# Weight buffers of 4096 bytes in place of 4288, and one input block of the mixer in three pieces in place of two

## The chip, the cores and the metric

The kernel runs on one core of a Trainium2 chip, in one launch. The metric is the device time of one execution in microseconds (us). The kernel before has three timed runs, with a median of 2028.21 us (2024.9 to 2028.38).

## The reference

Two layers of a streaming encoder work on 512 tokens of 1024 features, all in float32. A layer has three sublayers: a SwiGLU feed-forward step (FFN), a mixer, and a second FFN. In front of each sublayer the input is shifted and scaled by vectors that come from a conditioning vector `c`; behind each comes a gated residual and a LayerNorm.

```python
for l in range(DEPTH):                                   # DEPTH = 2
    h = modulate(x, mod[:, 0, 0], mod[:, 0, 1])
    y = swiglu_ffn(h, ffn1_w_in[l], ffn1_w_out[l])       # 1024 -> 2 x 2816 -> 1024
    x = layer_norm(ALPHA * x + 0.5 * mod[:, 0, 2] * y, ln_g[l, 0], ln_b[l, 0])
    h = modulate(x, mod[:, 1, 0], mod[:, 1, 1])
    proj = h @ mix_w_in[l]                               # 1024 -> 3084 columns
    ...                                                  # scan | attention | short convolution
    y = jnp.concatenate([y_ssd, y_fox, y_sc], axis=-1) @ mix_w_out[l]
    x = layer_norm(ALPHA * x + mod[:, 1, 2] * y, ln_g[l, 1], ln_b[l, 1])
    h = modulate(x, mod[:, 2, 0], mod[:, 2, 1])
    y = swiglu_ffn(h, ffn2_w_in[l], ffn2_w_out[l])
    x = layer_norm(ALPHA * x + 0.5 * mod[:, 2, 2] * y, ln_g[l, 2], ln_b[l, 2])
```

## The kernel before

**Products in three parts.** Every large operand is held as two float32r parts, a high one and a low one (the rest). One block of a product is three matmuls, in the helper `mm3`: the low part of the stationary operand by the high part of the moving one, then high by low, then high by high. The names tell the parts: `hi` and `li` are the high and low part of an FFN input weight, `ho` and `lo` of an output weight, `hm...` and `lm...` of a mixer weight, `hh` and `hl` of the sublayer's transposed input, `ah` and `al` of the FFN's activations.

Two kinds of product make up most of the work. In the input products (`pf` in the FFN, `pj...` in the mixer) the stationary operand is a 128x128 block of weights, and the moving one is 512 columns of `hh` or `hl`. The three matmuls of a block are, in this order, `pf<-hh,li`, `pf<-hl,hi` and `pf<-hh,hi` (the name behind the arrow is the moving operand, the last one the stationary). Eight blocks, 24 matmuls, fill one accumulator of 512 columns; I call these 24 a run of products. In the output products (`po`) and the gate of the mixer (`pz`) it is the other way round: the stationary operand is a block of the activations (or of `hh`, `hl`), the moving one 512 columns of weights: `po<-ho,al`, `po<-lo,ah`, `po<-ho,ah`. In the first pair of a later FFN and in two of the mixer's projections (`b`, `c`) a matmul has only 256 columns.

**Weights.** `load` (line 395) brings 1 MB of raw weights into one of two buffers (`rawp`); `split` (line 407) makes the high part on ScalarE (ACT) and the low part on VectorE (DVE), for one half of the block at a time, into one of six buffers of the pool `whp` and one of six of `wlp`. The six are taken in turn, so a new half waits until the products that read the half six places earlier are through. `WSZ` (line 35) is the number of float32 words of such a buffer: 1072, or 4288 bytes per partition. A half of a usual block needs 1024 words. The 1072 words are needed in one place: at the head of the mixer the columns of v, forget gate and dt (268 in all) are loaded in two pieces of 4 x 268 words each (lines 790 to 806, products `pv`).

**Where the operands lie.** All buffers are laid one behind the other in SBUF in the order of the pools. In the built program of the kernel before, the places per partition, modulo 512 bytes, are:

| operand | place of its buffers modulo 512 |
|---|---|
| `whp`, buffers 0 to 5 (`hi`, `ho`, `hm`) | 448, 128, 320, 0, 192, 384 |
| `wlp`, buffers 0 to 5 (`li`, `lo`, `lm`) | 64, 256, 448, 128, 320, 0 |
| `hh`, `hl`; `ah`, `al`; the other long-lived tiles | 192 |

The blocks inside a buffer lie at multiples of 512 bytes from its start, so that a matmul's operand has the place of its buffer. A low part lies 128 bytes behind its high part, modulo 512, in every pair of buffers. In pair 4 the high part has the place of `hh`, `hl`, `ah` and `al`; in pair 0 it lies 256 bytes from it, and in pairs 5, 3, 2 and 1 at 192, 320, 128 and 448 bytes behind it.

**Order.** TensorE (PE) runs its instructions in the order of the program, mostly that of the code; adaLN work (`ra`, `acc`) is spread between the weight units by `tick`. SyncE (SP) issues all loads of weights in order.

Of the kernel before, what the change touches and what calls it, by code (L numbers as in the profile page):

```python
# [15 lines left out]
P = 128  # L16
# [17 lines left out]
CR = (2.7, 1.3)  # L34
WSZ = 1072

# [5 lines left out]
class InOrder:  # L42
    """An engine whose instructions are issued in program order while it is on."""

# [16 lines left out]
def issue_after(tc, ins, prev):  # L61
    """Issue order on one engine."""
    tc.add_manual_dep(ins.ins, prev.ins.name,
                      mybir.DependencyInfo(mybir.DependencyClass.NoSync, mybir.DependencyReason.DATA),
                      reason="issue order")
# [3 lines left out]
def trunk(ctx, tc, x, c, ln_in_g, ln_in_b, ada_w, ada_b, ffn1_w_in, ffn1_w_out,  # L69
# [6 lines left out]

    const = ctx.enter_context(tc.tile_pool(name="const", bufs=1))
    rawp = ctx.enter_context(tc.tile_pool(name="rawp", bufs=2))
    adap = ctx.enter_context(tc.tile_pool(name="adap", bufs=2))
# [31 lines left out]

# [1 line left out]
    ident = const.tile([P, P], F32, name="ident")  # L113
# [4 lines left out]
    pool.memset(mhalf, -0.5)  # L118
# [1 line left out]
    cT = const.tile([P, KD], F32, name="cT")  # L120
# [32 lines left out]
    def columns(dst, rows):  # L153
        """[n, 128] to [128, n]."""
        n = rows.shape[0]
        ps = pb([P, n], f"pv_{dst.tensor.name}")
        pe.transpose(ps, rows, ident[0:n, 0:n])
        dve.tensor_copy(dst, ps)

# [1 line left out]
    identb = const.tile([P, P], BF16, name="identb")  # L161
# [51 lines left out]

# [1 line left out]
    gates = {}  # L215
# [6 lines left out]
    def ada_acc(l, col):  # L222
        """acc[p, f] = sum_k silu(c)[8p + k] * ada_w[l, 8p + k, col + f], row by row."""
        w = ada_w[l].rearrange("(p k) f -> p k f", k=KD)
# [15 lines left out]
    def acc_split(acc):  # L240
        """The high and low part of each half."""
        parts = []
        los = adap.tile([P, 2, 512], F32R, tag="ra", name="gl")
        for h in range(2):
            hi, lo = tmp([P, 512], "gh", F32R), los[:, h]
            act.activation(hi, acc[h], AF.Copy)
            dve.tensor_tensor(lo, acc[h], hi.bitcast(F32), ALU.subtract)
            parts.append((hi, lo))
        return parts

    def acc_sum(ps, hi, lo):
        """The sum over the partitions, on every partition."""
        pe.matmul(ps, onesr, hi, start=True, stop=False)
        pe.matmul(ps, onesr, lo, start=False, stop=True)
# [5 lines left out]
    def mod_finish(s, a, b, psc, pss):  # L260
        """Features a*128 to b*128: scale and shift folded with the LayerNorm in front."""
        l, j = divmod(s, 3)
# [38 lines left out]
    def ada_first(part, which):  # L301
        """The row blocks of the first sublayer's scale (1) or shift (0) for one range of features."""
        w = ada_w[0].rearrange("(p k) f -> p k f", k=KD)
# [13 lines left out]
    def sum_first(part, raws):  # L317
        """The sums over the row blocks, one vector instruction at a time."""
        n = FIRST[part][1] * P
# [50 lines left out]
    def begin(*gens):  # L370
        """Queue background work, to be spread over the 33 weight units of a half-step FFN."""
        pending.extend(gens)
        credit[0] = 0.0
        credit[1] = len(pending) and CR[0] if len(gens) > 2 else CR[1]
# [17 lines left out]

# [1 line left out]
    def load(w, c0, r0, k, n, name):  # L394
        """Rows r0 to r0 + 128 k, columns c0 to c0 + n, as [128, k, n]."""
        raw = rawp.tile([P, 2048], F32, tag="raw", name="r" + name)
# [6 lines left out]
    def split(v, name, prev=None):  # L403
        """One half unit, any view [128, a, b] of raw weights, as high and low parts."""
        a, b = v.shape[1], v.shape[2]
# [6 lines left out]
    def cols_unit(w, c0, name, prev=None):  # L412
        """256 columns of a [1024, .] matrix, two halves [128, 8, 128]."""
        v = load(w, c0, 0, KD, 256, name)
        return [split(v[:, :, j * P:(j + 1) * P], f"{name}_{j}", prev) for j in range(2)]

    def rows_unit(w, r0, c0, nk, name, prev=None):
        """128 nk rows by 512 columns, halves [128, 2, 512]."""
        v = load(w, c0, r0, nk, 512, name)
# [7 lines left out]

# [1 line left out]
    def ln_stat(t, h, st, piece=None):  # L429
        """Statistics of 512 columns, or of one half of them."""  # L430
        n = 2 * 512 // st.shape[1]
# [16 lines left out]
    def finish(t, st):  # L448
        """The last LayerNorm, stored."""
        mu, rs = ln_mr(st)  # L450
# [8 lines left out]
    def ln_norm(t, st):  # L459
        """xt[t] <- (xt[t] - mean) * rstd."""  # L460
        mu, rs = ln_mr(st)
# [4 lines left out]
    def modulate(s, t, qq=(0, 1), prev=None):  # L466
        """hT[:, :, t] = the transposed modulation of xt[t] for sublayer s."""
        ts = slice(t * P, (t + 1) * P)
# [22 lines left out]
    def modulate_first(kk, ps):  # L491
        """hT[:, kk, :] for the first sublayer; yields before the vector part."""
        hf = tmp([P, T], f"hf0_{kk}")
# [9 lines left out]
    def ln_in(t):  # L503
        """The first LayerNorm of one token tile; yields between its vector parts."""
        ln_stat(t, 0, st0[t])
# [9 lines left out]
    def start():  # L515
        """Up to the first pair of the first sublayer, by ranges of features."""
        for e in (pe, dve, act):
# [108 lines left out]
    def x_affine(s, eng):  # L626
        """xt = normalized * g + b of the LayerNorm in front of sublayer s."""
        ln_vectors(s)
# [6 lines left out]
    def fold(s, ps, t, h, first, half, a=0, b=512):  # L635
        """xt[t][:, h] <- (alpha *) xt + gate * (1/2) * ps, columns a to b."""
        hs = slice(h * 512 + a, h * 512 + b)
# [11 lines left out]

# [1 line left out]
    def by_token(ah, al):  # L651
# [52 lines left out]
    def out_proj(s, w_out, r0, acts, half, first, last):  # L704
        """x <- (alpha *) x + gate * (acts^T w_out); with last, on to the next sublayer's input."""
        n = len(acts)
# [43 lines left out]

# [1 line left out]
    def mixer(s, l):  # L752
        w_in, w_out = mix_w_in[l], mix_w_out[l]

        def feat(c0, name, epi, halves=False, between=None):
            """256 projected features, feature-major; epi(chunk, psum)."""
            us = cols_unit(w_in, c0, name)
# [31 lines left out]

        # v, forget-gate and dt columns together, token-major  # L790
        us = []
        for u in range(2):
            raw = rawp.tile([P, 2048], F32, tag="raw", name=f"rm{s}v{u}")
            v = raw[:, 0:4 * 268].rearrange("p (k f) -> p k f", f=268)
            rs = slice(u * 512, (u + 1) * 512)
            sp.dma_start(v[:, :, 0:260], w_in[rs, C_V:C_V + 260].rearrange("(k p) f -> p k f", p=P))
# [3 lines left out]
        for t in range(NT):  # L800
            ts = slice(t * P, (t + 1) * P)
            ps = pa([P, 268], f"pv{s}_{t}")
            for k in range(KD):
                wh, wl = us[k // 4]
                mm3(ps, hT[0][:, k, ts], hT[1][:, k, ts], wh[:, k % 4, :], wl[:, k % 4, :],
                    k == 0, k == KD - 1)
# [32 lines left out]

        # sums within a 128-token chunk: up to the token, of the whole chunk, after the token  # L840
        def decays(prev):
# [8 lines left out]

            # forget gate: minus its running sum, one row per head
            psf = pb([P, NT, 4], f"pcf{s}")
# [21 lines left out]

        # B token-major
        btok = []
# [9 lines left out]

        # token-major x * dt and x * d
        xdt, xd = [], []
# [13 lines left out]

        # gate z, token-major
        zs = []
# [22 lines left out]
        def ssd_decay(i):  # L927
            """M[s, e, l] = (C_l . B_s) exp(sum of a over s < . <= l) for l >= s, per group."""
            ts = slice(i * P, (i + 1) * P)
# [21 lines left out]
        def ssd_state(i):  # L951
            """The state after chunk i: [n, h, d]."""
            xw = tmp([P, 8, 64], f"xw{s}_{i}")
# [54 lines left out]

        # forgetting attention
        qT = [slot([P, 2, 256], F32, f"q{s}_{u}") for u in range(2)]  # L1010
# [6 lines left out]
        def k_epi(j, ps):  # L1017
            """Per head: the high part twice, and the low part over minus the sums of the forget gate."""
            for p in range(2):
# [11 lines left out]
        def attn(i):  # L1031
            """One block of 128 queries, two stages for each head."""
            n = (i + 1) * P
# [47 lines left out]

        # gated short convolution
        cS, uS, gT = [], [], []
# [56 lines left out]

# [1 line left out]

# [42 lines left out]
```

## Time and profile before

| | |
|---|---|
| median of three runs | 2028.21 us (2024.9 to 2028.38) |
| span of the profiled execution, first to last instruction | 2026.3 us |
| PE busy | 1980.4 us (98%) in 9462 matmuls |
| DVE, ACT, POOL busy | 1190.0 us, 688.5 us, 218.2 us |
| share of PE in the chain that ended last | 85% |
| granted TensorE clock, mean | 0.998 |

The page gives no time of the profiled execution beside its span. The span lies 1.9 us under the median of the timed runs and within their range. Matmuls are pipelined: the duration of one in the profile (some 390 ns) is longer than the distance from its start to the next one's (some 230 ns), so the pace is read from stretches with a known number of matmuls. The names in the profile leave out buffer numbers; which buffer a stretch uses follows from counting the halves through the six buffers in the order of the program.

### The profile page before, as it was taken

How to read it: one execution, taken by the hardware profiler on the slowest of the kernel's cores; microseconds unless marked ns; L12 is line 12 of the kernel's file. 1: busy time of each engine (PE TensorE's matmuls, PEld its weight loads, DVE VectorE, ACT ScalarE, POOL GpSimd, SP SyncE). 2: the span in 40 equal slices, each digit the busy share in tenths (PEclk: the TensorE clock that was granted, in tenths of full speed). 3: DMA queues.
4: the chain of work that ended last, by engine and by line, in shares of the span. 5: the costliest groups of instructions: out<-in, count | busy, mean ns of one | idle time of the engine just before them, and what ended most of it. 6: DMA issues, size and time to landing. Idle time of an engine off the chain costs nothing.

```text
span 2026.3 us, 23498 instructions
## 1 busy us (share of the span) xinstructions
PE 1980.4 (98%) x9462; PEld 1624.8 (80%) x9462; DVE 1190.0 (59%) x1728; ACT 688.5 (34%) x1092; POOL 218.2 (11%) x182
## 2 busy tenths in 40 slices
PE   5999999999999999999999999999999999999998
PEld 4777878898877888888898788888977798888887
DVE  8896663467666655543477757436666575433336
ACT  3332132164454422122152322323544453222220
POOL 0230000007000040000004000000350004000000
PEclk9999999999999999999999999999999999999999
DMA  9765552333211544432345746322322144223331
GB/s 322 232 208 208 177 166 73 95 92 117 83 63 53 182 155 158 149 106 92 104 162 173 240 157 235 104 84 81 122 80 73 53 137 136 102 84 103 104 104 42
DMA packets 178540, 263.98 MB, mean 130 GB/s; under 512 B 9612, under 2 KB 124672, under 8 KB 178432
## 3 DMA queue, kind: packets, MB, share of 16 engines
q1 hardware_dynamic: 173936, 254.97, 37.7%
q10 hardware_dynamic: 4496, 7.52, 1.2%
q8 instruction: 74, 1.21, 0.2%
q14 instruction: 34, 0.28, 0.0%
HBM read 260.37 MB, written 2.10 MB: 130 GB/s over the span
## 4 chain that ended last, share of the span: by engine, by line
PE 85%; DVE 7%; DMA 4%; ACT 2%; issue 1%; POOL 0%; POOLq 0%; SPq 0%; DVEq 0%; ACTq 0%
PE pf L52 42%; PE po L52 26%; DMA ra<-in_ada_w_dram 4%; DVE acc L52 2%; PE pz L52 2%; PE pv L52 1%; PE pfo L52 1%; PE ptr L52 1%; DVE li L52 1%; PE pjm1x L52 1%; PE pS L52 1%; DVE af L52 1%; PE py L52 1%; PE pjm1sx L52 1%; PE pjm4sx L52 1%
## 5 line engine op out<-in xcount | busy, mean ns | idle before, releaser
L52 PE MATMUL pf<-hh,li 128*128 128x512 f32 (+1 forms) x1504 | 574.5, 382 | 1.3 <-DVE li L52 1.0
L52 PE MATMUL pf<-hl,hi 128*128 128x512 f32 (+1 forms) x1504 | 571.2, 380 | 0.2 <-DVE hl L52 0.2
L52 PE MATMUL pf<-hh,hi 128*128 128x512 f32 (+1 forms) x1504 | 570.7, 379 | 0.0
L52 DVE TENSOR_TENSOR li<-ri,hi 128x1024 fp32r<-128x1024 f32 x176 | 224.0, 1278 | 187.4 <-ACT hi L52 187.2
L52 PEld LDWEIGHTS pf<-hh,li 128*128 128x128 f32 x1504 | 283.3, 188 | 58.5 <-DVE li L52 1.7
L52 PEld LDWEIGHTS pf<-hl,hi 128*128 128x128 f32 x1504 | 284.8, 189 | 56.1 <-DVE hl L52 0.8
L52 PEld LDWEIGHTS pf<-hh,hi 128*128 128x128 f32 x1504 | 283.5, 188 | 57.7
L52 ACT ACTIVATE hi<-ri 128x1024 fp32r<-128x1024 f32 x176 | 185.4, 1059 | 317.4 <-PE pf L52 203.7
L52 PE MATMUL po<-ho,al 128*128 128x512 f32 (+1 forms) x704 | 276.6, 393 | 0.0
L52 PE MATMUL po<-ho,ah 128*128 128x512 f32 (+1 forms) x704 | 275.3, 391 | 0.0
L52 PE MATMUL po<-lo,ah 128*128 128x512 f32 (+1 forms) x704 | 274.7, 390 | 0.0
L52 DVE TENSOR_TENSOR lo<-ro,ho 128x1024 fp32r<-128x1024 f32 x104 | 127.2, 1223 | 215.3 <-ACT ho L52 215.2
L52 ACT ACTIVATE ho<-ro 128x1024 fp32r<-128x1024 f32 x104 | 110.1, 1058 | 293.1 <-PE po L52 166.6
L52 DVE SCALAR_TENSOR_TENSOR acc<-ra,cT,acc 128x512 f32<-128x512 f32 x224 | 171.6, 810 | 62.2 <-DMA ra<-in_ada_w_dram 61.9
L445 POOL TENSOR_TENSOR rs<-ve,mhalf 128x1 f32<-128x1 f32 x28 | 17.3, 619 | 1296.8 <-DVE ve L52 1277.8
L52 PEld LDWEIGHTS po<-ho,ah 128*128 128x128 f32 x704 | 132.1, 188 | 30.6
L52 PEld LDWEIGHTS po<-lo,ah 128*128 128x128 f32 x704 | 132.3, 188 | 29.6
L52 PEld LDWEIGHTS po<-ho,al 128*128 128x128 f32 x704 | 132.2, 188 | 29.6 <-DVE dg L52 0.3
L52 ACT ACTIVATE sg<-pf 128x512 f32<-128x512 f32 x88 | 52.4, 595 | 293.9 <-PE pf L52 276.8
L52 DVE TENSOR_TENSOR af<-sg,pf 128x512 f32<-128x512 f32 x88 | 60.2, 685 | 150.2 <-PE pf L52 147.3
L52 ACT ACTIVATE hf<-ptr,modB,modA 128x128 f32<-128x128 f32 (+1 forms) x168 | 66.8, 486 | 97.2 <-PE ptr L52 81.7
L632 POOL TENSOR_TENSOR x<-x,lng 128x512 f32<-128x512 f32 x48 | 76.3, 1613 | 215.3 <-DMA lng<-in_ln_g_dram 211.1
(391 smaller groups left out, 2448.0 us busy)
## 6 DMA issues: line engine op xcount, KB each, us to landing
ri<-in_ffn_w_in_dram SPq DMA_DIRECT2D x88, 1024.0 KB, 5.0
ra<-in_ada_w_dram SPq DMA_DIRECT2D x128, 512.0 KB, 4.5
ro<-in_ffn_w_out_dram SPq DMA_DIRECT2D x40, 1024.0 KB, 5.0
ro<-in_mix_w_out_dram SPq DMA_DIRECT2D x8, 1024.0 KB, 4.9
rf<-in_ada_w_dram SPq DMA_DIRECT2D x8, 512.0 KB, 8.6
ro<-in_ffn_w_out_dram SPq DMA_DIRECT2D x8, 512.0 KB, 3.6
rf<-in_ada_w_dram SPq DMA_DIRECT2D x16, 192.0 KB, 7.0
gate<-in_ada_b_dram SPq DMA_DIRECT2D x12, 256.0 KB, 5.8
```

The source lines that it names most:

```text
L52: ins = f(*a, **k)
L445: pool.tensor_tensor(rs, ve, mhalf[:, 0:1], ALU.pow)
L632: eng.tensor_tensor(xh, xh, aff[s, "g", h], ALU.mult)
```

## The change

`WSZ` becomes 1024, so that each of the twelve buffers has 4096 bytes. The pools behind them move down by 2304 bytes. With this the places modulo 512 bytes become:

| operand | place modulo 512 before | after |
|---|---|---|
| `whp`, all buffers | 448, 128, 320, 0, 192, 384 | 448 |
| `wlp`, all buffers | 64, 256, 448, 128, 320, 0 | 448 |
| `hh`, `hl`, `ah`, `al`, other long-lived tiles | 192 | 448 |
| raw weights | 448 | 448 |
| `x`, constants | as they were | as they were |

Since 4 x 268 words don't fit any more, the v block of each mixer is loaded and split in three pieces of 3, 3 and 2 row blocks. A helper `shift` is added that nothing calls; comments and docstrings go.

```diff
-WSZ = 1072
+WSZ = 1024
...
+    def shift(name, words):
+
+        ctx.enter_context(tc.tile_pool(name=name, bufs=1)).tile([P, words], F32, name=name)
...
-        for u in range(2):
+        for u, (k0, nk) in enumerate(((0, 3), (3, 3), (6, 2))):
             raw = rawp.tile([P, 2048], F32, tag="raw", name=f"rm{s}v{u}")
-            v = raw[:, 0:4 * 268].rearrange("p (k f) -> p k f", f=268)
-            rs = slice(u * 512, (u + 1) * 512)
+            v = raw[:, 0:nk * 268].rearrange("p (k f) -> p k f", f=268)
+            rs = slice(k0 * P, (k0 + nk) * P)
...
-                wh, wl = us[k // 4]
-                mm3(ps, hT[0][:, k, ts], hT[1][:, k, ts], wh[:, k % 4, :], wl[:, k % 4, :],
+                wh, wl = us[k // 3]
+                mm3(ps, hT[0][:, k, ts], hT[1][:, k, ts], wh[:, k % 3, :], wl[:, k % 3, :],
```

The number and the shapes of PE's instructions stay the same. What moves stands at the head of the two mixers. On SP, at the head of the first mixer, the loads before (`rm...v` is the raw v block, `rm...b` and `rm...c` the raw blocks of the next two projections):

```order
L398 DMA ro_1536_1_8_2891<-in_ffn_w_out_dram 128x2x512
L796 DMA rm1v_3138<-in_mix_w_in_dram 128x4x260
L797 DMA rm1v_3138<-in_mix_w_in_dram 128x4x8
L796 DMA rm1v_3145<-in_mix_w_in_dram 128x4x260
L797 DMA rm1v_3145<-in_mix_w_in_dram 128x4x8
L398 DMA rm1b<-in_mix_w_in_dram 128x8x256
L398 DMA rm1c<-in_mix_w_in_dram 128x8x256
```

And after, on SP in the same place:

```order
L402 DMA ro_1536_1_8_2891<-in_ffn_w_out_dram 128x2x512
L800 DMA rm1v_3138<-in_mix_w_in_dram 128x3x260
L801 DMA rm1v_3138<-in_mix_w_in_dram 128x3x8
L800 DMA rm1v_3145<-in_mix_w_in_dram 128x3x260
L801 DMA rm1v_3145<-in_mix_w_in_dram 128x3x8
L800 DMA rm1v_3152<-in_mix_w_in_dram 128x2x260
L801 DMA rm1v_3152<-in_mix_w_in_dram 128x2x8
L402 DMA rm1b<-in_mix_w_in_dram 128x8x256
L402 DMA rm1c<-in_mix_w_in_dram 128x8x256
```

One more raw block passes through the two raw buffers: `rm1b` now takes the buffer of the second v piece, where it took that of the first.

On ACT, in the same place, the copies that make the high parts (`hm...`), among the modulation of the new input (`hf`, `hh`), before:

```order
L52 ACTIVATE hm1v_3148<-rm1v_3145 128x1072
L52 ACTIVATE hh_2703<-hf_1_1_3065 128x4x128
L52 ACTIVATE hm1b_3318<-rm1b 128x1024
L52 ACTIVATE hm1b_3322<-rm1b 128x1024
L52 ACTIVATE hf_2_0_3118<-ptr_2_0_3113,modB_822,modA_821 128x128 x4
```

And after, on ACT:

```order
L52 ACTIVATE hm1v_3148<-rm1v_3145 128x804
L52 ACTIVATE hh_2703<-hf_1_1_3065 128x4x128
L52 ACTIVATE hm1v_3155<-rm1v_3152 128x536
L52 ACTIVATE hf_2_0_3118<-ptr_2_0_3113,modB_822,modA_821 128x128 x4
L52 ACTIVATE hf_2_1_3130<-ptr_2_1_3125,modB_822,modA_821 128x128
```

The third v piece stands where the first half of `rm1b` stood, and both halves of `rm1b` come later. DVE, which makes the low parts, moves in the same way.

## Rows read from the trace of the kernel before

**Rows 1.** The page: span, and busy time, share and instructions of each engine.
```profile
span 2026.3 us, 23498 instructions
PE 1980.4 (98%) x9462; PEld 1624.8 (80%) x9462; DVE 1190.0 (59%) x1728; ACT 688.5 (34%) x1092; POOL 218.2 (11%) x182
```

**Rows 2.** Groups on PE by shape: count, busy us, mean ns, idle before.
```profile
L52 PE MATMUL pf<-hh,li 128*128 128x512 f32 x1312 | 520.4, 397 | 1.3 <-DVE li L52 1.0 <-ACT hh L52 0.3
...
L52 PE MATMUL po<-ho,al 128*128 128x512 f32 x694 | 273.8, 395 | 0.0
...
L52 PE MATMUL pf<-hh,li 128*128 128x256 f32 x192 | 54.1, 282 | 0.0
```

**Rows 3.** Stretch, us, PE busy, PEclk, DMA: input runs, pairs 5, 1, 3, 2, 0, 4.
```profile
906.02:911.51 5.49, 5.49 (x25) 1.00 0.34 103
911.51:917.00 5.49, 5.49 (x25) 1.00 0.55 183
917.00:922.57 5.57, 5.57 (x25) 1.00 0.32 101
922.57:928.17 5.60, 5.60 (x26) 1.00 0.25 87
928.17:933.72 5.55, 5.55 (x25) 1.00 0.30 96
939.22:944.76 5.54, 5.54 (x25) 1.00 0.27 92
sum 33.24, PE 33.24; mean PE 5.54
```

**Rows 4.** Same view: an earlier input run in pair 1; output products, pair 4.
```profile
882.82:888.41 5.59, 5.59 (x25) 1.00 0.31 105
368.06:373.65 5.59, 5.59 (x26) 1.00 0.26 92
```

**Rows 5.** Matmuls of the input run in pair 5: duration min/median/max.
```profile
L52 PE MATMUL pf<-hl,hi x8: 394/394/394, 906.2 to 911.1; 128*128 128x512 f32 x8
L52 PE MATMUL pf<-hh,hi x8: 388/388/388, 906.5 to 911.3; 128*128 128x512 f32 x8
L52 PE MATMUL pf<-hh,li x7: 392/392/392, 906.7 to 910.8; 128*128 128x512 f32 x7
```

**Rows 6.** The same of the input run in pair 4.
```profile
L52 PE MATMUL pf<-hl,hi x8: 389/389/389, 939.5 to 944.3; 128*128 128x512 f32 x8
L52 PE MATMUL pf<-hh,hi x8: 388/396/396, 939.7 to 944.5; 128*128 128x512 f32 x8
L52 PE MATMUL pf<-hh,li x7: 397/397/398, 939.9 to 944.1; 128*128 128x512 f32 x7
```

**Rows 7.** The same of the output stretch in pair 4.
```profile
L52 PE MATMUL po<-lo,ah x8: 393/395/395, 368.3 to 373.2; 128*128 128x512 f32 x8
L52 PE MATMUL po<-ho,ah x8: 388/392/393, 368.5 to 373.4; 128*128 128x512 f32 x8
L52 PE MATMUL po<-ho,al x7: 397/398/398, 368.7 to 372.9; 128*128 128x512 f32 x7
```

**Rows 8.** Stretches: half runs of 24 matmuls of 256 columns, pairs 4 and 3.
```profile
672.80:675.66 2.86, 2.86 (x26) 1.00 0.92 279
678.39:681.11 2.72, 2.72 (x26) 1.00 0.91 309
```

**Rows 9.** Timeline of ACT and DVE at the first mixer's head.
```profile
415.86 1.14 ACT L52 ACTIVATE hm1v<-rm1v 128x1072 fp32r<-128x1072 f32 x1
...
417.04 1.28 DVE L52 TENSOR_TENSOR lm1v<-rm1v,hm1v 128x1072 fp32r<-128x1072 f32 x1 [0.22 <-ACT hm1v L52]
```

**Rows 10.** First products there, and the load of `rm1c`.
```profile
L52 PE MATMUL pv<-hm1v,hl x32: 282/285/392, 420.6 to 433.4; 128*128 128x268 f32 x32
...
L52 PE MATMUL pjm1b<-hl,hm1b x32: 274/282/363, 433.8 to 446.8; 128*128 128x256 f32 x32
...
DMA to landing us min/median/max: 5.6/5.6/5.6
```

## The prediction

> **What bounds the kernel now.** I read the page first: of a span of 2026.3 us PE is busy for 1980.4 [rows 1], so that the end moves by what PE's matmuls take and by little else. DVE, the next engine, is at 59%. The second view groups PE's matmuls by shape [rows 2]. The reader should see two things there. The large groups have 128x512 operands, and nothing stops them: the idle time ahead of all 1312 `pf<-hh,li` is 1.3 us, 1.0 of it for `li`. So copying weights into the buffers is off the path, and an effect can only come from the pace of the matmuls themselves.
>
> That pace is the third view, PE's stretches [rows 3]. Each row is one run of 24 input matmuls with the same shapes, from its first start to the next run's first start; the granted clock is 1.00 in all, the upper level of 2.4 GHz. Still the runs take 5.49, 5.49, 5.57, 5.60, 5.55 and 5.54 us. The share of the DMA engines doesn't explain it: the run with the most traffic (0.55) is one of the two shortest, the longest has the least (0.25). What differs is the pair of weight buffers, so the place of the stationary operand beside the moving one. The mean is 33.24 / 144 = 230.8 ns a matmul, and the extremes are 228.8 (5.49 / 24) and 233.3 (5.60 / 24).
>
> The place is not all of it: a run in pair 1 takes 5.59 us in one case [rows 4] and 5.49 in another [rows 3]. So a run also remembers how it began.
>
> The fourth view is the single matmuls of two runs. In pair 5 the three kinds last 394, 388 and 392 ns, every one of them the same eight (or seven) times [rows 5]. This regularity tells me that it is no noise. In pair 4, where `hi` has the place of `hh` and `hl`, and `li` is 128 bytes off, `pf<-hl,hi` lasts 389 ns all eight times, the two others mostly 396 and 397 [rows 6]. A longer duration is a slower pace: the mean of pair 5's medians is 391.3 ns at 228.8 ns from start to start, that of pair 4's is 394.0 at 5.54 / 24 = 230.8. So a nanosecond of duration is about 0.75 to 1 ns of pace.
>
> **The change part by part.** I sum against the span of 2026.3 us and carry the difference over to the median, 2028.2; the page has no time of its own for what lies around the span.
>
> *Input products with 512 columns.* There are 3 x 1312 = 3936 in the FFNs [rows 2], and by the code 7 projections x 48 x 2 mixers = 672, together 4608. Afterwards every one of them has its stationary operand, the next stationary operand and the moving operand at one place. In the trace before, only `pf<-hl,hi` in pair 4 is in that position (the next matmul uses the same `hi`), and it lasts 389 [rows 6]. I take the gain from the pace: 230.8 now [rows 3]; 389 is 2.3 below pair 5's mean of 391.3, so 228.8 - 2.3 = 226.5 afterwards. One reserve: that matmul loads the same block of weights again for the next one, as two of three won't afterwards. Bounds: if the history of a run wins, nothing; if all fall to the slowest run's 233.3, a loss of 2.5 ns each, 11.5 us. Gain 4.3 ns x 4608 = 19.8 us, which I take, since that one row is the only one with the new position.
>
> *Products with moving weights.* 3 x 694 = 2082 in the FFNs [rows 2], 384 in the mixers' outputs and 192 in their gates by the code: 2658. Here the trace speaks against the change. The stretch in pair 4, where `ho` has the place of `ah` and `al`, is a slow one, 5.59 us [rows 4], or 232.9 ns. In it `po<-ho,ah`, with everything at one place up to the next matmul, lasts 392, while `po<-ho,al`, after which the moving operand goes to `lo` 128 bytes off, lasts 398 [rows 7]. Bounds: 389 as above would give 4.3 ns x 2658 = 11.4 us of gain; 232.9 for all would cost 2.1 ns x 2658 = 5.6 us. I take 1 ns of gain, since 392, the one row in the new position, is 0.7 below the mean of the six medians of rows 5 and 6 (392.7); 2.7 us.
>
> *Matmuls with 256 columns.* 3 x 192 = 576 in the FFNs [rows 2] and 384 in the mixers: 960. A half run takes 2.86 us in pair 4 and 2.72 in pair 3 [rows 8], 119.2 and 113.3 ns. The new position is nearest to pair 4. From the mean of the two, 116.3, that is 2.9 ns x 960 = 2.8 us of loss; the other way it would be the same gain. I take the loss.
>
> *The third v piece.* In each mixer ACT and DVE make one more copy and one more subtraction, over the same 2144 words in all; the two pieces before take about 1.14 and 1.28 us each [rows 9]. On the path stands this: the first `pv` starts at 420.6, and 3 x 32 = 96 of them take 12.8 us [rows 10], 0.13 each, so that the third piece, the last quarter of the rows, is needed 18 matmuls later, near 423.0. Before, the second piece is through DVE at 417.04 + 1.28 = 418.3; the third, half as wide, follows on the same engines in about 1.5 us, near 420. That is 3 us of cover. `rm1b` is loaded later, since its raw buffer is now freed by the second piece: some 418.3 + 5.6 for the load [rows 10] = 424, and two halves on ACT and DVE, near 428. Its main use begins at 433.8 [rows 10]. SP holds nothing else that is urgent behind it, `rm1c` alone, whose products come after 446.7. I take 0.3 us for both mixers together; if the cover fails, PE waits 1 to 2 us in each, so 3 us is the upper end, and nothing excludes a small gain.
>
> *Copies into the new buffers.* All operands of ACT's and DVE's splits move too. Both engines are hidden (1.3 us of idle in front of 1312 matmuls), so nothing.
>
> Sum: -19.8 - 2.7 + 2.8 + 0.3 = -19.4 us; 2028.2 - 19.4 = 2008.8, say 2009.
>
> **A rule against it.** Rows 3 and 6 show matmuls whose length goes with the place of their operands. The Trainium skill, page "SBUF — State Buffer", section "Who interferes with whom", gives PE two independent read ports, one for the moving operand and one for the loading of weights, and says that "PE and ACT never wait on anyone". By that rule alone the place could not matter, and the sum would be the 0.3 us of the mixers. The trace doesn't agree with it in this form, at 5.49 against 5.60 us for equal runs at one clock.
>
> **The rivals.**
>
> *The whole gain* (chance 0.25). With all operands alike, nothing pushes a run out of the short pattern, the output products reach 226.5 too, and 7266 matmuls win 4.3 ns: 31.2 us, less 2.8 for the 256 columns: 2000. For it: the steady 388 and 389 [rows 5, 6]. Against it: 392 for `po<-ho,ah` [rows 7].
>
> *No change* (chance 0.14). The pattern is set by how a run begins, not by the place; runs average out at 230.8 as before and the mixers cost 0.3 us: 2028.5. For it: pair 1 at both 5.49 and 5.59 [rows 3, 4]. Against it: the fixed order of the kinds in a run. The page "SBUF — State Buffer" of the Trainium skill, as read above, would also end here.
>
> *The new place is a bad one* (chance 0.12). Reading the moving operand and the next weights from one place modulo 512 makes them meet, and every run settles in the pattern of the slow output stretch (232.9 ns) or of pair 2 (233.3). Then 7266 x 2.1 to 2.5 ns = 15.3 to 18.2 us of loss, and 2.8 more: about 2047. For it: the slow stretch is just the one with `ho` at the place of `ah` and `al` [rows 4]. Against it: in that stretch the slow matmuls are those next to `lo`. It decides as soon as the mean pace goes above 230.8.
>
> **How the numbers follow.** My forecast has 0.49. All of it and of the whole gain is faster by more than 0.2% (4 us, about what a measurement of this kernel can tell from no change), which is 0.74; a small gain left of "no change" makes it 0.75. Same 0.12, slower 0.13. The range starts at 1994, below the whole gain, since 388 instead of 389 and three good cases of the 256 columns would take some 6 us more, and ends at 2031, past "no change" with 3 us for the mixers. Outside are most of the bad place (0.12) and a small remainder below. The forecast's own range is 2000 to 2018.
>
> **What would show it.** Right, if runs of 24 input matmuls take about 5.44 us whatever the buffers, with all three kinds near 389, and output stretches lie between 5.44 and 5.54. The mean of the `pf` groups should fall by some 4 ns, that of `po` by 1. Half runs should be at 2.86. At the mixers' head PE should show no new wait for `lm1v` or `lm1b`. Wrong, if runs still come in several lengths (no change), if they are all at 5.59 (a bad place), or if PE's pace falls as forecast and the span doesn't, which would put the loss into a wait that I priced at nothing.

## The result, and the profile after

The changed kernel takes 2010.45 us (median of four runs, 2004.11 to 2012.99), the kernel before 2027.5 us in the same comparison. The ratio is 0.9908, with a 95% interval of 0.989 to 0.9925. The profiled run is the longest of the four, at 2012.99 us, so that the traces show a little less than the medians' 17.05 us. Against the span of before [rows 1] its span is shorter by 15.1 us, PE's busy time by 22.4:

```profile
span 2011.2 us, 23510 instructions
...
PE 1958.0 (97%) x9462; PEld 1629.4 (81%) x9462; DVE 1189.0 (59%) x1730; ACT 689.2 (34%) x1094; POOL 217.2 (11%) x182
```

So 7.3 us of what PE saved came back as time in which PE has nothing to do. The groups of matmuls by shape, as in [rows 2]:

```profile
L52 PE MATMUL pf<-hh,li 128*128 128x512 f32 x1312 | 514.1, 392 | 1.3 <-DVE li L52 1.0 <-ACT hh L52 0.3
...
L52 PE MATMUL po<-ho,al 128*128 128x512 f32 x694 | 270.5, 390 | 0.3 <-DVE af L52 0.3
...
L52 PE MATMUL pf<-hh,li 128*128 128x256 f32 x192 | 54.8, 285 | 0.0
```

Both kinds with 512 columns last 5 ns less (397 and 395 before), and the 256-wide ones 3 ns more (282). The six input runs of [rows 3], found by counting matmuls from the start; columns as there:

```profile
900.89:906.33 5.44, 5.44 (x26) 1.00 0.36 104
906.33:911.77 5.44, 5.44 (x26) 1.00 0.57 186
911.77:917.21 5.44, 5.44 (x26) 1.00 0.31 94
917.21:922.65 5.44, 5.44 (x26) 1.00 0.29 99
922.65:928.09 5.44, 5.44 (x26) 1.00 0.31 86
933.53:938.97 5.44, 5.44 (x26) 1.00 0.31 76
sum 32.64, PE 32.64; mean PE 5.44
```

One length, where there were five. The run and the output stretch of [rows 4], and the two half runs of [rows 8]:

```profile
878.22:883.66 5.44, 5.44 (x25) 1.00 0.31 90
368.69:374.13 5.44, 5.44 (x25) 1.00 0.26 82
671.83:674.71 2.88, 2.88 (x27) 1.00 0.85 266
677.59:680.47 2.88, 2.88 (x27) 1.00 0.88 296
```

The output stretch has gone from 5.59 to 5.44, and the two half runs are now alike, both a little longer than the longer of before. The single matmuls of the run that stood in [rows 5]:

```profile
L52 PE MATMUL pf<-hh,li x9: 389/389/389, 900.9 to 906.3; 128*128 128x512 f32 x9
...
```

And those of the output stretch of [rows 7]:

```profile
L52 PE MATMUL po<-ho,ah x9: 389/389/389, 368.5 to 373.9; 128*128 128x512 f32 x9
...
```

The kinds left out show the same three figures. Every kind is at the 389 that one kind alone had in [rows 6].

What came back is seen in PE's waits. Each row: what PE waited with, for what, us in total, times, longest. After:

```profile
PE pm L52 <- ACT gh L52: 10.0, 4, 3.8
...
PE pm L52 <- DVE vT L52: 3.6, 1, 3.6
PE pv L52 <- DVE hl L52: 1.4, 2, 1.2
```

The same view of before, which has no wait of `pv` for `hl`:

```profile
PE pm L52 <- ACT gh L52: 6.2, 4, 3.1
...
PE pm L52 <- DVE vT L52: 2.2, 1, 2.2
```

`pm` are the sums of the adaLN vectors in `ada_ss`; `gh` is the high part of `acc`, which DVE adds up from eight loads `ra`. Against these loads PE comes to the sums earlier now: a load lands 4.0 us after its issue in the median, and took 4.5 before. The longest of these waits on PE's timeline (start, duration, then the idle time before it and its releaser):

```profile
1137.93 0.39 PE L52 MATMUL pf<-hl,hi 128*128 128x512 f32 x1
1142.12 0.80 PE L52 MATMUL pm<-gh,onesr 128*128 128x512 f32 x1 [3.80 <-ACT gh L52]
1142.71 0.63 PE L52 MATMUL pf<-hh,hi 128*128 128x512 f32 x1
1143.14 0.63 PE L52 MATMUL pm<-gh,onesr 128*128 128x512 f32 x1
```

After it matmuls start 0.43 us apart (1142.71 to 1143.14), which is the lower level of the clock, 1.2 GHz. The stretch from the start of that wait, after, and the like stretch before (us, busy time of PE, PEld, DVE, ACT, POOL, granted clock, DMA share, GB/s):

```profile
1137.90:1150.00 12.10, 8.30 (x26) 6.20 (x25) 9.70 (x17) 2.43 (x5) 0.00 (x0) 0.72 0.57 175
```

```profile
1146.70:1158.80 12.10, 9.02 (x30) 6.40 (x29) 9.69 (x18) 3.41 (x5) 0.00 (x0) 0.86 0.59 201
```

26 matmuls fit into the 12.1 us where 30 did, and the clock is lower for longer (a mean of 0.72, where it was 0.86).

To close the sum I took the distance from each matmul's start to the next one's in both traces. An excess over the usual pace counts as a gap:

| | before | after | change, us |
|---|---|---|---|
| 512-wide, at 2.4 GHz, ns each | 231.2 | 227.1 | -30.4 |
| 512-wide at 1.2 GHz, some 426 ns, number | 18 | 40 | +4.3 |
| 256-wide, us in all | 128.2 | 131.3 | +3.1 |
| gaps, us in all | 66.1 | 73.9 | +7.8 |
| span | 2026.3 | 2011.2 | -15.1 |

(7338 x 4.14 ns = 30.4; 22 x 195 ns = 4.3; the rest is 0.1.)

### The profile page after: what moved, and what is told of

Its sections match the earlier page's. It is cut to its first block, busy times and chain, and to the rows that moved or that the text cites. A ratio compares the mean times of both kernels' runs of the same rounds, so it can differ in the third digit from the quotient of the medians.

```text
span 2011.2 us, 23510 instructions
## 1 busy us (share of the span) xinstructions
PE 1958.0 (97%) x9462; PEld 1629.4 (81%) x9462; DVE 1189.0 (59%) x1730; ACT 689.2 (34%) x1094; POOL 217.2 (11%) x182
## 4 chain that ended last, share of the span: by engine, by line
PE 84%; DVE 7%; DMA 6%; ACT 1%; issue 1%; SPq 0%; POOL 0%; POOLq 0%; DVEq 0%; ACTq 0%
PE pf L52 40%; PE po L52 25%; DMA ra<-in_ada_w_dram 4%; DVE acc L52 2%; PE pz L52 2%; DMA rf<-in_ada_w_dram 1%; DVE li L52 1%; PE pfo L52 1%; PE pjm4x L52 1%; PE pjm1x L52 1%; PE pS L52 1%; PE py L52 1%; PE ptr L52 1%; DVE af L52 1%; PE pm L52 1%
## 5 line engine op out<-in xcount | busy, mean ns | idle before, releaser
L52 DVE SCALAR_TENSOR_TENSOR acc<-ra,cT,acc 128x512 f32<-128x512 f32 x224 | 170.8, 806 | 67.7 <-DMA ra<-in_ada_w_dram 67.2
```

Of the source, the lines that this page charges most:

```text
L52: ins = f(*a, **k)
```

## The experiments

The theory is that the pace of a matmul depends on how its operands lie relative to each other, and that about 10 us of the gain were given back at the adaLN sums: 5.2 in longer waits for `gh` and `vT`, 4.3 in lower clock. The first four runs shared a chip, as did the next four, and the three after that. Each ratio is to the kernel before on the same chip.

**The v pieces without the new places**

```diff
-WSZ = 1024
+WSZ = 1072
```

> The kernel after, with buffers of 1072 words again: the three v pieces stay, the places are those of the kernel before. Theory (the gain is the place of the operands): the pace of the 512-wide matmuls stays spread over 225 to 237 ns with a mean near 231, and the time is that of before, 2026 to 2031 us. Rival (the gain comes from the new order at the mixers' heads): about 2010 us. Rival (the third piece is what gave back a part of the gain): 2030 to 2036 us, with a wait of PE at the mixers' heads.

Measured: 2032.14 us, ratio 1.0014 (1.0003 to 1.0025). Four of its runs of 24:

```profile
905.04:910.60 5.56, 5.56 (x25) 1.00 0.36 106
...
916.15:921.65 5.50, 5.50 (x26) 1.00 0.31 95
...
927.19:932.80 5.61, 5.61 (x26) 1.00 0.31 91
938.36:943.96 5.60, 5.60 (x25) 1.00 0.31 92
```

The mean pace is 231.4 ns, so the gain is the places. The time is 1 us above the theory's range and inside that of the rival in which the third piece gives a part back; PE waits 1.1 us for `hl` here. The six runs show still more. The third v piece takes a pair of buffers of its own. In the built program the six buffers are handed out again in the order in which they come free, not strictly in turn, so that the runs that stood in pairs 5, 1, 3, 2, 0 and 4 in [rows 3] are now in pairs 3, 0, 1, 4, 2 and 5 (the four rows: 3, 1, 2 and 5). Five of the pairs keep their length to 0.01 us: pair 3 has 5.56 (5.57 before), pair 0 5.55 (5.55), pair 1 5.50 (5.49), pair 4 5.54 (5.54), pair 2 5.61 (5.60). In these the length goes with the buffers and not with the place in the program. But pair 5 has 5.60 in place of 5.49, and over all runs of this kernel pairs 1 and 5 come at both lengths, so that with unlike places the start of a run counts too.

**Activations 64, 128 and 256 bytes away from the weights**

```diff
     wlp = ctx.enter_context(tc.tile_pool(name="wlp", bufs=NW))
+    shift("gap", 16)
     lp = ctx.enter_context(tc.tile_pool(name="lp", bufs=NLONG))
```

These are 16 words; the next two kernels have 32 and 64.

> The kernel after with 64 bytes left free between the weight buffers and the tiles behind them: hi and li stay at one place, hh, hl, ah and al lie 64 bytes further. Theory (all operands must lie alike): the lock at 227 ns is lost, the runs of 24 go to 5.5 to 5.6 us, and the time to 2025 to 2045 us. Rival (only that hi and li lie alike matters, because a matmul's stationary block and the next one's are then read alike): 5.44 us in all runs, and 2010 us.

> The same with 128 bytes. Theory: lock lost; the slow patterns of before had operands 128 bytes apart, so 231 to 233 ns, 2030 to 2045 us. Rival (hi and li alike is enough): 2010 us. If the loss grows with the distance, this is slower than the 64 bytes; if it is lost or kept as a whole, equal to them.

> The same with 256 bytes: alike modulo 256, unlike modulo 512. Theory with modulo 512: lost like the others, 2025 to 2045 us. Theory with modulo 256 (in the kernel before, pairs 4 and 0, whose operands differ by 256 bytes, showed the same pattern of distances from start to start): the lock at 227 ns is kept, 2008 to 2013 us. Rival (hi and li alike is enough): 2010 us too, but then the two runs before this one also.

Measured: 2029.63 (ratio 1.0015, 1.0 to 1.003), 2036.83 (1.0038, 1.0024 to 1.0053) and 2006.0 us (0.9897, 0.9871 to 0.9924). An input run, an output stretch and a half run of each, first with 64 bytes:

```profile
911.41:916.91 5.50, 5.50 (x26) 1.00 0.54 182
367.59:373.19 5.60, 5.60 (x25) 1.00 0.28 91
672.76:675.59 2.83, 2.83 (x27) 1.00 0.83 252
```

With 128:

```profile
913.39:918.96 5.57, 5.57 (x26) 1.00 0.53 181
367.19:372.79 5.60, 5.60 (x25) 1.00 0.30 84
673.43:676.27 2.84, 2.84 (x26) 1.00 0.76 245
```

And with 256:

```profile
900.99:906.43 5.44, 5.44 (x25) 1.00 0.56 187
363.16:368.60 5.44, 5.44 (x26) 1.00 0.25 85
666.50:669.38 2.88, 2.88 (x26) 1.00 0.85 265
```

That `hi` and `li` lie alike is not enough: with 64 and 128 bytes the whole gain is gone, and 128 are the worse (a mean of 232.6 ns for the 512-wide matmuls, against 231.0 with 64). With 256 all of it stays, down to the half runs. So what counts, as far as these distances tell, is the place modulo 256 bytes, and the 512 of the change's description is more than was needed. Of the two kinds, output stretches suffer more from 64 bytes (5.60) than most input runs (5.50).

One thing more shows with 64 bytes. All six pairs lie alike there, and still the input runs have two lengths. Of the 153 runs without a pause in them 127 last 5.49 to 5.51 us, and 26 last 5.60. The length changes only where something else, such as the adaLN sums, stands between two runs. Two runs, both in pair 4:

```profile
90.55:96.15 5.60, 5.60 (x26) 1.00 0.82 263
301.56:307.06 5.50, 5.50 (x26) 1.00 0.27 93
```

So with unlike operands what ran before has a part in the length, even when all buffers have the same place. In the kernel after, 148 of 153 such runs last 5.44 us, and none more than 5.47.

**All operands at another common place**

```diff
     adap = ctx.enter_context(tc.tile_pool(name="adap", bufs=2))
+    shift("gap", 16)
     whp = ctx.enter_context(tc.tile_pool(name="whp", bufs=NW))
```

> The kernel after with 64 bytes left free ahead of the weight buffers, so that weights and activations lie at 0 modulo 512, all of them alike. Theory (only the place of one operand relative to the other counts): the lock at 227 ns stays, 2006 to 2013 us. Rival (448 modulo 512 is a good place in itself): the lock is lost, 2025 us or more.

Measured: 2006.97 us, ratio 0.9906 (0.9891 to 0.992).

```profile
909.94:915.38 5.44, 5.44 (x26) 1.00 0.30 92
366.44:371.88 5.44, 5.44 (x25) 1.00 0.31 79
```

Weights and activations at 0 modulo 512 do the same as at 448, so the place itself has no part in it, as far as these two tell.

**Low parts alone moved, by 128 bytes: pair 4 of before, six times**

```diff
     whp = ctx.enter_context(tc.tile_pool(name="whp", bufs=NW))
+    shift("gap", 32)
     wlp = ctx.enter_context(tc.tile_pool(name="wlp", bufs=NW))
+    shift("gap2", 96)
     lp = ctx.enter_context(tc.tile_pool(name="lp", bufs=NLONG))
```

> The kernel after with 128 bytes left free between high and low weight buffers: hi, hh, hl, ah and al alike at 448, li and lo 128 bytes behind, as in pair 4 of the kernel before, now in all six pairs. Theory (one unlike operand is enough to lose the lock): input runs near 5.54 us and output stretches near 5.59, as pair 4 had them, and 2028 to 2035 us. Rival (hi at the place of the activations is what matters, since two of three matmuls then read alike): 2010 to 2018 us.

Measured: 2025.62 us, ratio 0.9997 (0.9988 to 1.0007).

```profile
911.01:916.56 5.55, 5.55 (x26) 1.00 0.55 183
367.36:372.85 5.49, 5.49 (x25) 1.00 0.29 88
```

One unlike operand of three loses the input runs' gain, and most of that of the output products (229.9 ns, where before has 231.1 and after 227.1). The time is 2.4 us below the theory's range. The input run is as pair 4 had it (5.54), the output stretch isn't: 5.49, where [rows 4] has 5.59. The 5.59 on which I sized a term was the stretch's history as well, not its place alone. The kernel before says so itself: its ten whole output stretches in pair 4 last from 5.49 to 5.60 us.

**The adaLN sums one run later**

The generators yield `HOLD` in place of `TICK` behind `acc_split`, and `ffn` keeps a tick that would emit the sums until the next run of products has been written:

```diff
-                    tick()
+                    if held[0]:
+                        late += 1
+                    else:
+                        tick()
...
+                    while late:
+                        late -= 1
+                        tick()
+                        if held[0]:
+                            break
```

> The kernel after, with one change of order: where the sums of an adaLN vector (pm, pg) stood ahead of a run of 24 input products, they come behind it, some 5.4 us later on PE; nothing else is left out or added. Theory (a part of the gain was given back, since the waits of PE for gh grow when the products are shorter, and the clock falls behind the longest): PE's waits for gh, 10.0 us in the kernel after, go below 2, the gaps ahead of the adaLN sums shrink by 12 to 15 us, the number of 512-wide matmuls at the lower clock falls from 40 to 20 or fewer (4 us), and the time is 1992 to 1999 us. Rival (the waits move to the next place, because DVE and the loads of ra end the chain): 2007 to 2012 us, with new waits for gh or for the tiles of the next sublayer.

> The same order with buffers of 4288 bytes, that is, the places of the kernel before and three v pieces. Theory: the same order wins less here, because the waits ahead of the adaLN sums were shorter at the slower pace (gaps of 16.6 us in all with buffers of 4288 bytes, 23.1 in the kernel after, 4.3 of it at the kernel's start in both): 8 to 11 us off the 2032 of the run with three v pieces alone, 2021 to 2024 us, and between this and the run with 4096 bytes the whole gain of the place shows, 27 to 31 us. Rival (the order wins the same in both, so that nothing was given back by it): 2015 to 2019 us, and a distance of 20 to 22 us as between the two kernels without it.

Measured: 2017.59 us (0.9954, 0.9939 to 0.9969) and 2038.0 us (1.0059, 1.0036 to 1.0083). The edit made both kernels slower, which neither side expected. Their distance of 20.4 us is the one that the rival of the second kernel named, but it decides nothing, since PE's waits for `gh` are now long in both (16.5 and 16.6 us). In the first, PE's wait and DVE's group of sums (its idle time is the last part):

```profile
PE pm L53 <- ACT gh L53: 16.5, 6, 5.2
```

```profile
L53 DVE SCALAR_TENSOR_TENSOR acc<-ra,cT,acc 128x512 f32<-128x512 f32 x224 | 168.9, 800 | 77.6 <-DMA ra<-in_ada_w_dram 77.5
```

A held tick also holds back the loads of `ra` that it would have issued, and DVE's idle time for `ra` is 77.5 us where the kernel after has 67.2 (below). My edit had moved the consumer and its supply together. This agrees with the rival's half of the story, that the loads end the chain, and I followed that with three more kernels. The chain of waits of the kernel after, ahead of the longest wait for `gh`, shows the same:

```profile
1127.01 5.73 DMA ra<-in_ada_w_dram
...
1132.76 1.43 DVE acc L52 x2
...
1134.21 5.03 DMA ra<-in_ada_w_dram
...
1139.33 1.20 DVE acc L52 x2
...
1141.44 0.64 ACT gh L52
```

A load of `ra` starts when DVE is through with one of the two buffers, and takes 5.7 and 5.0 us to land here.

**Half of the `ra` traffic**

```diff
-            raw = adap.tile([P, D], F32, tag="ra", name=f"ra{l}_{col}_{k}")
-            sp.dma_start(raw, w[:, k, col:col + D])
+            if k % 2 == 0:
+                raw = adap.tile([P, D], F32, tag="ra", name=f"ra{l}_{col}_{k}")
+                sp.dma_start(raw, w[:, k, col:col + D])
```

> The kernel after without every second load of adaLN weights (ra): each loaded block is used for two steps of the sum, so that ACT, DVE and PE do the same work in the same order and half of the ra traffic, 32 MB, is left out (the adaLN vectors come out as other numbers). Theory (PE waits for gh because the loads of ra, two buffers deep, can't keep up with the faster products): the 10.0 us of waiting for gh go below 3, the 512-wide matmuls at the lower clock from 40 to 20 or fewer, and the time to 1991 to 1998 us. Rival (the chain of the sums on DVE and ACT sets it, not the loads): the waits stay at 7 us or more, 2005 to 2011 us.

> The same cut of the ra traffic with buffers of 4288 bytes, that is, the places of the kernel before and three v pieces. Theory: without the waits for ra the distance between this and the run with 4096 bytes is the whole gain of the pace, 30 us for the 512-wide matmuls less 3 for the 256-wide, 26 to 29 us, with this one at 2018 to 2025. Rival (nothing was given back, the loads of ra don't come into it): the distance stays at about 20 us, as between the runs with all of ra.

Measured: 2001.8 us (0.9876, 0.9861 to 0.9891) and 2028.32 us (1.0003, 0.9994 to 1.0013). No wait for `gh` is left in either, and 12 matmuls each are at the lower clock. Both are longer than expected, since the earlier sums now stand on DVE ahead of one `li`:

```profile
119.25 0.80 PE L52 MATMUL pf<-hh,li 128*128 128x512 f32 x1 [8.57 <-DVE li L52]
```

That wait is in both (8.6 and 8.0 us), so their distance tells: 26.5 us, inside the 26 to 29 expected, not the rival's 20. In the traces it is 31.1 us for the 512-wide products, less 2.6 for the 256-wide ones and 2.1 of gaps.

**A third buffer for `ra`**

```diff
-    adap = ctx.enter_context(tc.tile_pool(name="adap", bufs=2))
+    adap = ctx.enter_context(tc.tile_pool(name="adap", bufs=3))
...
-NTMP = 9
+NTMP = 8
```

> The kernel after with three buffers for the ra blocks in place of two (8 buffers for short-lived tiles in place of 9, to make room); all work is done, all places modulo 512 stay. Theory (the loads of ra wait for one of two buffers): the loads start earlier, PE's waits for gh fall from 10.0 us to 5 or less, 1999 to 2006 us. Rival (the loads of ra are late because the DMA engines are busy with them and the weights, 0.84 of the time ahead of the longest wait): the waits stay, 2006 to 2012 us.

Measured: 1996.39 us, ratio 0.9847 (0.9832 to 0.9862), the fastest kernel here and 2.6 us below the expected range. The waits for `gh` are gone, and of those for the adaLN sums one is left:

```profile
PE pm L52 <- DVE vT L52: 4.5, 1, 4.5
```

DVE's sums wait 38.5 us for `ra`; the row of this run, then that of the kernel after:

```profile
L52 DVE SCALAR_TENSOR_TENSOR acc<-ra,cT,acc 128x512 f32<-128x512 f32 x224 | 172.7, 823 | 38.8 <-DMA ra<-in_ada_w_dram 38.5
```

```profile
L52 DVE SCALAR_TENSOR_TENSOR acc<-ra,cT,acc 128x512 f32<-128x512 f32 x224 | 170.8, 806 | 67.7 <-DMA ra<-in_ada_w_dram 67.2
```

Against the kernel after, the gaps fall from 73.9 to 61.9 us and the matmuls at the lower clock from 40 to 16. The pace is the same, 227.1 ns.

**The smaller pool alone**

```diff
-NTMP = 9
+NTMP = 8
```

> The kernel after with 8 buffers for short-lived tiles in place of 9, the other half of the edit of the run with three ra buffers, by itself. Theory (the third ra buffer is what took the waits away): 2006 to 2013 us as the kernel after, with some 9 to 10 us of waiting for gh. Rival (the smaller pool changed the order of the tiles and took the waits away): 1994 to 1999 us, without the waits for gh.

Measured: 2012.75 us, ratio 0.9918 (0.9901 to 0.9936).

```profile
PE pm L52 <- ACT gh L52: 11.0, 4, 3.3
```

So the third buffer took the waits away; between the two ratios, 0.9918 and 0.9847, lie 14 us. The DMA engines, at 0.84 of the time ahead of the longest wait, were not the limit that the rival made of them.

## Why the prediction was right, and where it was not

The time, 2009 against 2010.45, was right, and so was its cause. But two errors of some 8 and 12 us in opposite directions, with smaller ones, stand behind the small difference. That they cancel is luck.

*Input products: right.* Forecast 226.5 ns each, measured 227.0 (231.4 before, from start to start): -20.4 us where -19.8 stood. Runs at 5.44 us whatever the buffers, and 389 for all kinds, came as written. The step from one kind in pair 4 to all of them carried.

*Products with moving weights: the term that was mis-sized.* I took 1 ns, from the 392 of `po<-ho,ah`, and measured 4.0 (231.1 to 227.1): -10.6 us in place of -2.7. The 392 [rows 7] stood for the new position in my working, but its neighbours in the same stretch were still unlike, and the run with the low parts alone moved shows that very stretch at 5.49 us with its operands equally far apart. The 392 held the history of the stretch, then, and one stretch was too few. For the input products I had trusted the like matmul in [rows 6]; here the bound from that same row, -11.4, was near the truth. In the pace, the rival of the whole gain was right. (The two kinds add up to 31.0 us where the table has 30.4, by where the line between pace and gap is drawn.)

*256 columns: right.* Forecast +2.8, measured +3.1.

*The third v piece: right in its bounds.* Neither `lm1v` nor `lm1b` made PE wait. The cost is in `hl` of the new input, which comes later on DVE: 1.4 us, where I had 0.3 and an upper end of 3.

*The waits: a term that stood at nothing.* The sum had no term for work that doesn't speed up with PE. PE reaches the adaLN sums earlier against the loads of `ra`, and it waits longer for them. Gaps of +7.8 us (1.4 of it the v piece) and +4.3 of lower clock make 12.1. This is read from the longest of the four runs; the shortest is 8.9 us faster and has no trace. I had named this case as what would make the forecast wrong (a wait that was priced at nothing), and gave it neither a term nor a chance. The waits of before show where to look: the adaLN sums were already waits of PE there, 6.2 us for `gh` and 2.2 for `vT`, which became 10.0 and 3.6, while the waits at the kernel's start (15.4 us for `af`, 6.0 for `x`) stayed as they were. The two kernels with half of the `ra` traffic show the gain without the waits for `gh`, 26.5 us. The one with three buffers lies 31 us below the kernel before, more than the pace gives, because it also loses waits that the kernel before had (gaps of 61.9 us, where before has 66.1). The kernel before with three buffers was not run.

*The rivals.* "No change" and "a bad place" fall with the one length of 5.44. The Trainium skill, page "SBUF — State Buffer", section "Who interferes with whom", has PE wait on nobody there. By that rule, as the prediction reads it, the runs with 0, 64 and 128 bytes between the operands would be alike; those shown are at 5.44, 5.50 and 5.57 us, so in this kernel the measurement decides against it.

Not settled: which mechanism in the reading of operands makes the place count. The runs show at which distances (256 bytes leave the pace as it is, 64 and 128 don't) and how much, not why.

## What to carry to other kernels

Where one long chain of matmuls bounds a kernel, compare equal runs of it by the buffers that they use: several sharp lengths at full clock point to the places of the operands, as they did here, and buffers in rotation hide it in a mean. Make the size of every rotating buffer a multiple of 256 bytes and give the other operands the same place modulo 256, then look at shapes of another width, which may want the opposite. When PE becomes faster, list the waits that it already has: those for work that doesn't speed up with it can grow (6.2 to 10.0 us here), and a longer one may cost the clock as well. A third buffer for loads of 512 KB was worth 14 us here.

## What the runs showed of the hardware

- The pace of 512-wide fp32r matmuls went with the operands' places modulo 256 bytes: 227.0 ns with all alike or 256 bytes apart, 229.7 (input) and 233.3 (output) at 64 bytes, 232.6 at 128.
- 256-wide ones go the other way: 119.9 ns with all alike, 117.8 at 64 bytes for the input products, 116.8 in the mixture before.
- With all operands alike modulo 256 the input runs have one length, 5.44 us. With unlike ones what ran before has a part in it: pair 5 shows 5.49 and 5.60 us in two kernels, pair 1 5.49 and 5.59 in one, and with 64 bytes between weights and activations in all six pairs the runs last 5.49 to 5.51 or 5.60.
- In the kernel after, 6 to 12 matmuls at the lower clock follow four gaps ahead of the adaLN sums (starts 2.20 to 4.19 us apart), but none follows another of 2.60 us, at 1258.8. What decides is not shown. Kernels with the same pace differ by this: the kernel after, the one with 256 bytes and the one at another common place have 40, 15 and 26 such matmuls, and profiled spans of 2011.2, 2004.4 and 2006.1 us.
